# A third pair chunk in the gating stage, and later places for steps of the norms and of the conditioning sums

## The chip, the cores and the metric

The kernel runs on one core of one Trainium2 chip. The metric is the device time of one execution in microseconds (us); a smaller number is better. Of several executions the median is given.

## What is computed

The reference is one step of a two-layer streaming encoder on two inputs, a prompt of 1024 rows and a sample of 32 rows, all 1024 wide and in float32. In short, with the parts that this change touches:

```
mod = silu(c) @ w_ada[i] + b_ada[i]          # conditioning: shifts, scales, gates
h   = rmsnorm(x, g0) * (1 + sc1) + sh1
z   = gelu(h @ w_in);  u, v = split(z)        # 1024 -> 2 x 2048
v   = rmsnorm(v, g_v)
s   = einsum('gij,bnjgd->bnigd', w_s * mask, v) + b_s   # 8 groups, blocks of 128 rows
mix = (u * s) @ w_out                         # 2048 -> 1024   ("gating stage", layer 0)
x   = x + gt1 * rmsnorm(mix, g1)
h   = rmsnorm(x, g2) * (1 + sc2) + sh2
x   = x + gt2 * rmsnorm(square(relu(h @ w_up)) @ w_down, g3)   # 1024 -> 4096 -> 1024
```

Layer 1 has a pooling mixer in place of the gating. Outputs are the two results, and the state rows that the next step needs.

## The kernel before, in words

**Tiles.** The 1056 rows lie in three tiles, with rows on the free axis and features on the partitions: tiles 0 and 1 have 384 prompt rows each, tile 2 has 256 prompt rows and the 32 sample rows (288). `hh[t]`, `hl[t]` hold a tile's normalised input as two float32r halves, high and low, and every weight is split likewise: ScalarE rounds the high part (`wh`, line 592 or, in `w_split`, line 546), VectorE subtracts to get the low part (`wl`, through the helper at line 80). One product is then three matmuls: high by high, high by low, low by high (lines 1134 to 1136).

**The gating stage** (lines 1466 to 2043) works by groups. A group has 256 of the 2048 columns of u, that is two blocks of 128. An ordinary item (`sgu_item`) takes two groups for one tile: four products `up` (8 x 3 matmuls each), Gelu on ScalarE, for each group the 12 small matmuls of `spatial`, the gating on VectorE, the rounding `split` (lines 1453 to 1455), and later `down`: eight blocks of output, 4 x 3 matmuls each, which `accumulate` adds into `acc[t]` (the first one for a tile is copied by ScalarE). `down` is put on the list `pending` and given out after the first `up` of the item that follows.

**Pair chunks.** `upair_item` (chunk p has groups 2p and 2p+1) does tiles 0 and 1 together with seven products of half size where eight would be needed (`pair_item`, line 1667). It needs combinations of the weights' quarters (`quads`, line 550: from two weight loads come A1, S31, S24 and A22, with four VectorE passes over 128 x 512 and three and a half splits where the ordinary way has two) and combinations of the input's quarters (`combo`), which `u_sums` (line 1341) makes once, as a filler. Its last part, four steps that write over the first half of `hh[0]` and `hl[0]`, opens when the pair chunks begin ("h0"). For each half chunk the seven products run in a fixed order: A1, S31, S24, S24, S31, A1, A22; ScalarE copies four sums out of PSUM and VectorE makes three additions. The `down` of a pair chunk has 192 matmuls of 384 columns.

**Order.** `mixes` lists the ordinary items with their tiles, `UPAIRS` the pair chunks. Before: groups 4, 5 and then 6, 7 for tile 0; pair chunks 0 and 1 (groups 0 to 3, tiles 0 and 1); groups 0, 1 and then 2, 3 for tile 2; groups 4, 5 for tiles 1 and 2; groups 6, 7 for tiles 1 and 2. When the pair chunks are done, tile 0 is complete, and its norm, residual and next norm run beside the items that follow (`mix_to_ffn`, line 1912).

**One stream of loads.** All weights and the conditioning matrix come by one list, `stream`, in order, each load 512 KB into one of three `raw` buffers. `some_ada(n)` puts n loads of the conditioning matrix into the list; VectorE multiplies and adds these up (`do_ada`, line 654), and after every fourth a small matmul folds the sum over the partitions (`turn_sums`, line 683; `fold_lag` says how much later in the planner's time). Split weights have 16 places of 128 x 1024, two for a weight; six of them (`R`) are lent to the combinations until the pair chunks end.

**A planner.** While the program is written out, `time["pe"]` and `time["dve"]` count estimated TensorE and VectorE time. `weave` gives out the next steps of the stream and of the `fillers` (norms, residuals, sums) by them. A filler that yields a number waits for so many planned us. `Stat` is a norm's sum of squares: `split_sum` (line 956) makes its two halves, one on ScalarE; `finish` (line 1000) waits 3.0 planned us in the gating stage and 1.2 later, then gives out the ones-products `pn` (line 1005) and two ScalarE steps (lines 1009, 1010). Each engine works off its own list in order; `tc.issue_after(x)` keeps what its block gives out behind instruction x in the list of that engine. In the feed-forward part, `ffn_item` (line 1646) has Relu (line 1662), square (1664) and `split` on ScalarE for each `up`.

Of the kernel before, what the change touches and what calls it, by code (L numbers as in the profile page):

```python
# [11 lines left out]
AF = mybir.ActivationFunctionType  # L12
# [4 lines left out]
D = 1024  # L17
# [18 lines left out]
def tile_stream_encoder_step(  # L36
# [26 lines left out]
    act = nc.scalar.activation  # L63
# [6 lines left out]
    def tick(us):  # L70
        time["pe"] += us
        time["dve"] = max(time["dve"], time["pe"] - 4.0)
# [33 lines left out]
    def acc_tile(t):  # L106
# [19 lines left out]
        out=quad, in_=ident.rearrange("p (c m) -> p m c", m=32), op=ALU.add, axis=AX.X  # L126
# [4 lines left out]
    epsT = const.tile([P, 1], F32, name="eps")  # L131
# [15 lines left out]
    def ps_dn(name):  # L147
        return psum.tile([P, 512], F32, tag="pd", bufs=3, name=name)

    def ps_ms(name):  # L150
        return psum.tile([P, 512], F32, tag="pm", bufs=3, name=name)

    def t_m(name):
        return work.tile([P, 384], F32, tag="m", bufs=3, name=name)
# [191 lines left out]
    def w_groups(n):  # L346
        gs, _ = mixes[n]
        for g in gs:
            for k in range(2):
                f = 2 * g + k  # L350
                add_w(
                    ("u", n, g, k),
                    sgu_w_in[0][:, f * P : (f + 1) * P].rearrange("(k p) f -> p k f", p=P),
                    (8, P),
                )
        for q in range(2):
            for g in gs:
                add_w(
                    ("o", n, g, q),
                    sgu_w_out[0][g * 256 : (g + 1) * 256, q * 512 : (q + 1) * 512].rearrange(  # L360
                        "(k p) d -> p k d", p=P
                    ),
                    (2, 512),
                )

    def w_upair(p):
        for j in range(4):
            f = 4 * p + j
            add_w(
                ("up", ("u", p), j),  # L370
                sgu_w_in[0][:, f * P : (f + 1) * P].rearrange("(k p) f -> p k f", p=P),
                (8, P),
                ("one", "two")[j % 2],
            )
        for q in range(4):
            add_w(
                ("dn", ("u", p), q),
                sgu_w_out[0][p * 512 : (p + 1) * 512, q * 256 : (q + 1) * 256].rearrange(
                    "(j p) d -> p j d", p=P
                ),  # L380
                (4, 256),
            )
# [31 lines left out]
    every = list(range(NT))  # L414
# [5 lines left out]
    passes += [(1, c, PAIR, 1) for c in range(1, 8)]  # L420
    passes += [(1, c, [NT - 1], 2) for c in (0, 2, 4, 6)]
    LEND_AT = (("v", 1, 3), ("up", 0, 0))
    UPAIRS = (0, 1)

    rest = []

    def some_ada(n):
        for _ in range(min(n, len(rest))):
            add, l, j = rest.pop(0)
            add(l, j)  # L430
# [20 lines left out]
        some_ada(8)  # L451
    rest += [(add_wide, 1, j) for j in (*range(8, 16), *range(8), *range(16, 48))]

    mixes = [((4, 5), every[:1]), ((6, 7), every[:1]), ((0, 1), every[2:]), ((2, 3), every[2:])]
    mixes += [((4, 5), every[1:]), ((6, 7), every[1:])]
    for n in range(len(mixes)):
        w_groups(n)
        if n == 1:
            for p in UPAIRS:
                w_upair(p)  # L460
                some_ada(3)
        if n > 3:
            some_ada(5)
    for n, (l, c, tiles, m) in enumerate(passes):
        if tiles == PAIR:
            w_chunk(n, (1 if c < 3 else 2) if l else (5 if c == 1 else 6) if c < 7 else 1)
# [13 lines left out]
    landed = {}  # L480
    LANDING = 5.0
    last_copy = [None]

    def behind_copy():
        return ExitStack() if last_copy[0] is None else tc.issue_after(last_copy[0])
# [238 lines left out]
    fold_lag = [3.0]  # L724
# [165 lines left out]
    def finish(tag):  # L890
        while any(f[0] == tag for f in fillers):
            pull(True)
        time["pe"] = max(time["pe"], time["dve"] - 3.0)
# [26 lines left out]
    class Stat:  # L920
# [34 lines left out]

        def split_sum(self, sq):
            a, b = (x[:, : self.n] for x in self.parts)
            act(out=a, in_=sq, func=AF.Identity, bias=epsT)
            stt(out=b, in0=sq, scalar=epsT, in1=a.bitcast(F32), op0=ALU.add, op1=ALU.subtract)

        def square(self, k, src=None):
# [37 lines left out]

        def finish(self, out):  # L1000
            n = self.n
            yield 3.0 if gating_now[0] else 1.2
            pn = ps_ms(f"pn_{self.tag}")
            for i, x in enumerate(self.parts):
                mm(pn[:, :n], onesr, x[:, :n], start=i == 0, stop=i == 1)
            tick(0.4)
            q = t_m(f"q_{self.tag}")[:, :n]
            r = work.tile([P, 384], F32, tag="rr", bufs=2, name=f"r_{self.tag}")[:, :n]
            act(out=r, in_=pn[:, :n], func=AF.Abs_reciprocal_sqrt, scale=1.0 / D)
            act(out=q, in_=r, func=AF.Square)  # L1010
            yield 2.5
            stt(out=q, in0=pn[:, :n], scalar=-0.5 / D, in1=q, op0=ALU.mult, op1=ALU.mult)
            stt(out=r, in0=q, scalar=1.5, in1=r, op0=ALU.add, op1=ALU.mult)
            out.append(r)
            yield False


    gating_now = [True]
# [218 lines left out]
    with tc.manual_schedule():  # L1237
# [63 lines left out]
        ps = ps_ms("pv0_5")  # L1301
# [105 lines left out]
    for p, b in v_order:  # L1407
        ps = ps_dn(f"pv{p}_{b}")
# [42 lines left out]
            pending.pop(0)()  # L1451

    def split(dst_hi, dst_lo, src, n):
        act(out=dst_hi[:, :n], in_=src[:, :n], func=AF.Copy)  # L1454
        tt(out=dst_lo[:, :n], in0=src[:, :n], in1=dst_hi[:, :n].bitcast(F32), op=ALU.subtract)

    def accumulate(t, d, ps, first):
        n = ncol[t]
        if first:
            act(out=A(t, d), in_=ps[:, :n], func=AF.Copy)  # L1460
        else:
            tt(out=A(t, d), in0=A(t, d), in1=ps[:, :n], op=ALU.add)
# [113 lines left out]
    def sgu_item(p, t, mix, after):  # L1576
        gs, tiles = mixes[p]
        last = t == tiles[-1]
        n = ncol[t]
        hid = []  # L1580

        def put(g, k, s):
            a, b = t_hid("h", f"ush{g}_{t}_{k}"), t_hid("l", f"usl{g}_{t}_{k}")
            split(a, b, s, n)
            hid.append((a, b))

        inputs, factors, spatial, gate = gating(t, mix, put)
        us = []

        def up(g, k):  # L1590
            if k == 0:
                inputs(g)
            ps = ps_up(f"pu{g}_{t}_{k}")
            products(ps, n, up_terms(("u", p, g, k), t))
            if k == 0:
                factors(g)
            if last:
                w_finish(("u", p, g, k))
            u = t_m(f"u{g}_{t}_{k}")
            act(out=u[:, :n], in_=ps[:, :n], func=AF.Gelu_apprx_tanh)  # L1600
            us.append(u)

        def down():
            for d in range(KB):
                ps = ps_dn(f"po{gs[0]}_{t}_{d}")
                terms = []
                for j, (a, b) in enumerate(hid):
                    wh, wl = need_w(("o", p, gs[j // 2], d // 4))
                    o = (j % 2) * 512 + (d % 4) * P
                    terms.append((wh[:, o : o + P], wl[:, o : o + P], a[:, :n], b[:, :n]))  # L1610
                products(ps, n, terms)
                accumulate(t, d, ps, gs[0] == (4 if t == 0 else 0))
                if d == 0 and after is not None:
                    st = Stat(t, f"rs_{t}")
                if after is not None:
                    st.square(d)
                if last and d % 4 == 3:
                    for g in gs:
                        w_finish(("o", p, g, d // 4))
                weave(d % 2)  # L1620
            if after is not None:
                after(st)

        for j in range(4):
            up(gs[j // 2], j % 2)
            if j % 2 == 1:
                gate(gs[j // 2], spatial(gs[j // 2]), us)
            weave(2 if len(tiles) == 1 else 1)
            if j == 0:
                flush()  # L1630
        pending.append(down)

    more_hid = [None, 0]
# [78 lines left out]
    def pair_item(p, after, ends, gate=None):  # L1712
# [115 lines left out]
        def down():  # L1828
            sts = {}
            for q in range(4):  # L1830
                wh, wl = need_w(("dn", p, q))
                for t in tiles:
# [5 lines left out]
                    for d, ps in two:  # L1838
                        if wait == 4:
                            products(ps, n, [term(wh, wl, t, j, d) for j in range(4)])  # L1840
                        accumulate(t, d, ps, gate is not None and c == UPAIRS[0] and t > 0)
                        if t in ends:
# [146 lines left out]
    def upair_item(p):  # L1989
# [30 lines left out]
        gate["hook"] = hook  # L2020
        pair_item(("u", p), to_ffn0, [0] if p == UPAIRS[-1] else [], gate)

    def upairs():
        u_open.append("h0")
        need_w(("up", ("u", UPAIRS[0]), 0, "A1"))
        state["kept"] = 2
        for p in UPAIRS:
            upair_item(p)
# [4 lines left out]
        acc[NT - 1] = acc_tile(NT - 1)  # L2033

    for p, (gs, tiles) in enumerate(mixes):
        if p == 2:
            upairs()
        mix = {g: sgu_group(g) for g in gs}
        for t in tiles:
            sgu_item(p, t, mix, to_ffn0 if gs[-1] == 7 and t > 0 else None)  # L2040

    gating_now[0] = False
    sgu_stack.close()
    late = pool("late")

# [337 lines left out]
```

## Time and profile before

| | |
|---|---|
| three runs | 2097.35, 2098.18, 2099.37 us; median 2098.18 |
| the profiled execution | 2097.82 us, of which the span of instructions is 2096.0 |
| TensorE busy | 2075.2 us, 99% of the span |
| VectorE busy | 1636.7 us, 78% |
| ScalarE busy | 1060.3 us, 51% |
| granted TensorE clock | 0.999 |
| bytes moved | 303.91 MB, a mean of 145 GB/s |

The stages, by the first and last instructions of each in the trace: the v half ends at 222 us; ordinary items for tile 0 until the first pair chunk's first product at 278.1; pair chunks until 432.2; ordinary items until 608, where the first feed-forward product starts; from 676 on the pair chunks of the feed-forward part.

How to read it: PE is TensorE, PEld its weight loads, DVE is VectorE, ACT is ScalarE, SP issues most DMAs. Matmuls overlap, so the durations of single matmuls sum to more than the time that they take. "Idle before" is time in which an engine had nothing running, with what ended it.

### The profile page before, as it was taken

To read this page: it belongs to the slowest core of one execution; us is meant where nothing else is said; L and a number is where in the kernel's file an instruction comes from. 1 tells how busy PE (TensorE), PEld (TensorE's weight loads), DVE (VectorE), ACT (ScalarE), POOL (GpSimd) and SP (SyncE) were. 2 spreads that over 40 slices of the span, in tenths; PEclk is the share of its full clock that TensorE was granted. 3 is DMA by queue.
4 is the path that set the end of the run, shared out by engine and by line. 5 is a ranking of instruction groups with operands and counts; after the bars stand their busy time and mean duration, and the time that the engine had idled before them with its cause. 6 is when DMAs were issued, how large, how long until landed. Compare 5 with 4: busy or idle time off the path is not lost.

```text
span 2096.0 us, 32878 instructions
## 1 busy us (share of the span) xinstructions
PE 2075.2 (99%) x12742; PEld 2004.8 (96%) x12742; DVE 1636.7 (78%) x2953; ACT 1060.3 (51%) x1902; POOL 22.3 (1%) x44
## 2 busy tenths in 40 slices
PE   8999999999999999999999999999999999999998
PEld 6878999999999999999999999999999999999998
DVE  6799786889789998888868989896867654569554
ACT  5633443454247643344446766675435443365555
POOL 0000000000000000000000000000000000001100
PEclk9999999999999999999999999999999999999999
DMA  8585534365444443343424667643223221148863
GB/s 296 164 264 181 185 109 131 116 208 181 139 128 138 131 136 111 121 131 111 131 83 141 206 195 240 192 142 98 91 76 113 84 81 59 53 125 230 204 178 93
DMA packets 410737, 303.91 MB, mean 145 GB/s; under 512 B 47022, under 2 KB 373974, under 8 KB 410580
## 3 DMA queue, kind: packets, MB, share of 16 engines
q1 hardware_dynamic: 409652, 300.52, 47.4%
q8 instruction: 100, 1.64, 0.3%
q0 software_dynamic: 896, 1.28, 0.2%
q14 instruction: 57, 0.47, 0.1%
q10 hardware_dynamic: 32, 0.01, 0.0%
HBM read 271.09 MB, written 30.66 MB: 144 GB/s over the span
## 4 chain that ended last, share of the span: by engine, by line
PE 88%; DVE 7%; DMA 2%; ACT 2%; issue 1%; SPq 0%; DVEq 0%; ACTq 0%
PE pg L1135 11%; PE pg L1134 11%; PE pg L1136 11%; PE pf L1134 4%; PE pf L1136 4%; PE pf L1135 4%; PE pfa L1758 3%; PE pfa L1760 3%; PE pfa L1759 3%; PE pv L1160 2%; PE pv L1162 2%; PE pv L1161 2%; PE po L1134 2%; PE po L1135 2%; PE po L1136 2%; PE pu L1134 2%
## 5 line engine op out<-in xcount | busy, mean ns | idle before, releaser
L1134 PE MATMUL pg<-fh,wh_dn 128*128 128x384 f32 (+1 forms) x960 | 311.4, 325 | 1.4 <-ACT fh L1454 1.0
L1135 PE MATMUL pg<-fl,wh_dn 128*128 128x384 f32 (+1 forms) x960 | 310.4, 323 | 0.1
L1136 PE MATMUL pg<-fh,wl_dn 128*128 128x384 f32 (+1 forms) x960 | 309.9, 323 | 0.0
L80 DVE TENSOR_TENSOR acc<-acc,pg 128x384 f32<-128x384 f32 (+1 forms) x272 | 143.8, 533 | 106.0 <-PE pg L1136 105.4
L80 DVE TENSOR_TENSOR wl_dn<-raw,wh_dn 128x1024 fp32r<-128x1024 f32 x136 | 166.0, 1221 | 71.2 <-ACT wh_dn L592 43.0
L80 DVE SCALAR_TENSOR_TENSOR aa<-raw,csil,aa 128x512 f32<-128x512 f32 (+1 forms) x364 | 208.4, 619 | 6.3 <-DMA raw<-in_w_ada_dram 5.8
L1134 PE MATMUL pf<-hh,wh_up 128*128 128x288 f32 (+1 forms) x632 | 192.3, 305 | 0.0
L1135 PE MATMUL pf<-hl,wh_up 128*128 128x288 f32 (+1 forms) x632 | 191.1, 302 | 0.0
L1136 PE MATMUL pf<-hh,wl_up 128*128 128x288 f32 (+1 forms) x632 | 190.8, 302 | 0.0
L1134 PEld LDWEIGHTS pg<-fh,wh_dn 128*128 128x128 f32 x960 | 180.1, 188 | 3.0 <-ACT fh L1454 1.6
L592 ACT ACTIVATE wh_dn<-raw 128x1024 fp32r<-128x1024 f32 x136 | 143.7, 1057 | 75.2 <-PE pf L1135 34.0
L1135 PEld LDWEIGHTS pg<-fl,wh_dn 128*128 128x128 f32 x960 | 180.2, 188 | 1.0 <-DVE fl L80 0.6
L1136 PEld LDWEIGHTS pg<-fh,wl_dn 128*128 128x128 f32 x960 | 180.2, 188 | 0.0
L592 ACT ACTIVATE wh_up<-raw 128x1024 fp32r<-128x1024 f32 x79 | 83.6, 1058 | 79.0 <-PE pg L1135 46.0
L1136 PEld LDWEIGHTS pf<-hh,wl_up 128*128 128x128 f32 x632 | 118.9, 188 | 0.3 <-DVE wl_up L80 0.3
L1135 PEld LDWEIGHTS pf<-hl,wh_up 128*128 128x128 f32 x632 | 118.6, 188 | 0.5
L1134 PEld LDWEIGHTS pf<-hh,wh_up 128*128 128x128 f32 x632 | 118.5, 187 | 0.6 <-ACT wh_up L592 0.2
L80 DVE TENSOR_TENSOR wl_up<-raw,wh_up 128x1024 fp32r<-128x1024 f32 x79 | 96.4, 1220 | 28.7 <-ACT wh_up L592 28.7
L1134 PE MATMUL pg<-fx,wh_dn 128*128 128x288 f32 (+1 forms) x352 | 109.4, 311 | 0.2 <-ACT fx L1454 0.2
L1764 ACT ACTIVATE a<-pfa 128x384 f32<-128x384 f32 x84 | 40.9, 487 | 133.6 <-PE pfa L1760 133.5
L1135 PE MATMUL pg<-fx,wh_dn 128*128 128x288 f32 (+1 forms) x352 | 108.3, 308 | 0.0
L1136 PE MATMUL pg<-fx,wl_dn 128*128 128x288 f32 (+1 forms) x352 | 108.0, 307 | 0.0
(825 smaller groups left out, 5675.4 us busy)
## 6 DMA issues: line engine op xcount, KB each, us to landing
raw<-in_ffn_w_up_dram SPq DMA_DIRECT2D x136, 512.0 KB, 4.0
raw<-in_ffn_w_down_dram SPq DMA_DIRECT2D x136, 512.0 KB, 4.1
raw<-in_w_ada_dram SPq DMA_DIRECT2D x90, 512.0 KB, 4.2
raw<-in_sgu_w_in_dram SPq DMA_DIRECT2D x48, 512.0 KB, 4.4
raw<-in_sgu_w_out_dram SPq DMA_DIRECT2D x32, 512.0 KB, 3.6
xd<-acc SPq DMA_DIRECT2D x8, 1536.0 KB, 8.4
xo_r<-xd SPq DMA_DIRECT2D x32, 384.0 KB, 4.5
vd<-vt SPq DMA_DIRECT2D x32, 256.0 KB, 3.8
```

The lines of the kernel that those rows point to most:

```text
L80: return op(out, *args, **kw)
L592: act(out=wh, in_=r, func=AF.Copy)
L1134: mm(ps[:, :n], wh, rh, start=i == 0, stop=False)
L1135: mm(ps[:, :n], wh, rl, start=False, stop=False)
L1136: mm(ps[:, :n], wl, rh, start=False, stop=i == last)
L1160: mm(ps[:m, :], a_h, wh[:, o : o + 512], start=k == 0, stop=False)
L1161: mm(ps[:m, :], a_h, wl[:, o : o + 512], start=False, stop=False)
L1162: mm(ps[:m, :], a_l, wh[:, o : o + 512], start=False, stop=k == KB - 1)
L1758: mm(ps[:, :n], wh[:, o], rh, start=first and k == 0, stop=False, skip_group_check=True)
L1759: mm(ps[:, :n], wh[:, o], rl, start=False, stop=False, skip_group_check=True)
L1760: mm(ps[:, :n], wl[:, o], rh, start=False, stop=k == HK - 1, skip_group_check=True)
L1764: i = act(out=x, in_=ps[:, :n], func=AF.Copy)
```

## The change

Chunk 2 (groups 4 and 5, tiles 0 and 1) becomes a pair chunk. The ordinary items are now: 6, 7 for tile 0 before the pair chunks; then 0, 1, then 2, 3, then 4, 5 for tile 2; then 6, 7 for tiles 1 and 2. Behind each pair chunk's weights come four conditioning loads (three before), behind the last ordinary item's weights four (five behind each of the last two before): 16 in either kernel. `split` remembers its ScalarE rounding, and the ScalarE steps of `split_sum` and `finish` are given out behind the latest one. In the gating stage `finish` waits 5.0 planned us where it waited 3.0. From the end of the gating stage the conditioning folds wait 2.0 planned us where they waited 0.3. The flags for the first accumulation and for the start of the pair chunks follow the new order.

```diff
-    UPAIRS = (0, 1)
+    UPAIRS = (0, 1, 2)
...
-    mixes = [((4, 5), every[:1]), ((6, 7), every[:1]), ((0, 1), every[2:]), ((2, 3), every[2:])]
-    mixes += [((4, 5), every[1:]), ((6, 7), every[1:])]
+    mixes = [((6, 7), every[:1])] + [((g, g + 1), every[2:]) for g in (0, 2, 4)]
+    mixes += [((6, 7), every[1:])]
     for n in range(len(mixes)):
         w_groups(n)
-        if n == 1:
+        if n == 0:
             for p in UPAIRS:
                 w_upair(p)
-                some_ada(3)
-        if n > 3:
-            some_ada(5)
+                some_ada(4)
+        if n == 4:
+            some_ada(4)
...
+    last_hidden = [None]
+
+    def behind_hidden():
+        return ExitStack() if last_hidden[0] is None else tc.issue_after(last_hidden[0])
...
         def split_sum(self, sq):
             a, b = (x[:, : self.n] for x in self.parts)
-            act(out=a, in_=sq, func=AF.Identity, bias=epsT)
+            with behind_hidden():
+                act(out=a, in_=sq, func=AF.Identity, bias=epsT)
...
         def finish(self, out):
             n = self.n
-            yield 3.0 if gating_now[0] else 1.2
+            yield 5.0 if gating_now[0] else 1.2
...
-            act(out=r, in_=pn[:, :n], func=AF.Abs_reciprocal_sqrt, scale=1.0 / D)
-            act(out=q, in_=r, func=AF.Square)
+            with behind_hidden():
+                act(out=r, in_=pn[:, :n], func=AF.Abs_reciprocal_sqrt, scale=1.0 / D)
+                act(out=q, in_=r, func=AF.Square)
...
     def split(dst_hi, dst_lo, src, n):
-        act(out=dst_hi[:, :n], in_=src[:, :n], func=AF.Copy)
+        i = act(out=dst_hi[:, :n], in_=src[:, :n], func=AF.Copy)
+        last_hidden[0] = i.ins
...
-                accumulate(t, d, ps, gs[0] == (4 if t == 0 else 0))
+                accumulate(t, d, ps, gs[0] == (6 if t == 0 else 0))
...
-        if p == 2:
+        if p == 1:
             upairs()
...
     gating_now[0] = False
+    fold_lag[0] = 2.0
```

## The prediction

> **What bounds the kernel now.** I read the page first (busy times, chain), then a table of stretches, then TensorE's waits.
>
> ```profile
> span 2096.0 us, 32878 instructions
> PE 2075.2 (99%) x12742; PEld 2004.8 (96%) x12742; DVE 1636.7 (78%) x2953; ACT 1060.3 (51%) x1902; POOL 22.3 (1%) x44
> ...
> PE 88%; DVE 7%; DMA 2%; ACT 2%; issue 1%; SPq 0%; DVEq 0%; ACTq 0%
> ```
>
> TensorE is busy for 99% of the span, and 88% of the chain that ended last is its own. A change helps by giving it fewer matmuls or by closing one of its few gaps, and hurts by opening new ones. Stretches of the gating stage:
>
> ```profile
> core 0: us, PE busy (x) PEld busy (x) DVE busy (x) ACT busy (x) POOL busy (x), PEclk, DMA share, GB/s
> 220.70:297.20 76.50, 76.50 (x463) 75.16 (x462) 63.33 (x129) 35.16 (x57) 0.00 (x0) 1.00 0.51 158
> 297.20:363.17 65.97, 65.97 (x399) 65.90 (x398) 49.45 (x90) 25.92 (x45) 0.00 (x0) 1.00 0.38 118
> 329.89:363.17 33.28, 33.28 (x193) 33.28 (x193) 23.43 (x36) 9.78 (x16) 0.00 (x0) 1.00 0.45 137
> 432.00:517.00 85.00, 83.19 (x598) 82.12 (x597) 75.62 (x146) 46.38 (x70) 1.25 (x4) 1.00 0.67 209
> ```
>
> Up to the end of the pair chunks (432 us) TensorE has no gap in these stretches; behind them it loses 1.8 us of 85, while VectorE is busy for 75.6. The third row after the heading is the `down` of a pair chunk: 192 matmuls of 384 columns (and the end of one before) in 33.28 us, one per 0.1733 us. That is the price of a matmul here; the durations (334 ns in the trace) overlap and can't be summed. TensorE's gaps from all its waits:
>
> ```profile
> PE pg L1134 <- ACT fh L1454: 1.0, 1, 1.0
> PE pn_r_0x L1005 <- ACT sc_r_0x L958: 0.9, 1, 0.9
> ...
> PE pfa L1758 <- ACT a L1764: 0.7, 2, 0.5
> PE ada L710 <- DVE part L696: 0.6, 2, 0.3
> ```
>
> The first, second and fourth are those that the later steps bear on.
>
> **The change part by part.** *Third pair chunk.* For groups 4 and 5 and tiles 0 and 1, `up` was 2 tiles x 4 blocks x 24 = 192 matmuls; seven products for each of two halves are 14 x 12 = 168. `down`, `spatial` and the weight transposes keep their numbers. 24 fewer at 0.1733 us: **-4.16 us**. [...]
>
> *What it costs VectorE in the pairs.* Rows of the groups over the whole trace and over the first pair chunk:
>
> ```profile
> L80 DVE TENSOR_TENSOR raw<-raw 128x512 f32<-128x512 f32 x64 | 44.0, 687 | 0.9
> ...
> L80 DVE SCALAR_TENSOR_TENSOR aa<-raw,csil,aa 128x512 f32<-128x512 f32 x10 | 6.9, 745 | 0.0
> ```
>
> Two halves x (four passes of 0.69 + one and a half splits and three additions at 1.2 and 0.55, by rows below) = 12.4 us more VectorE work for the groups that change over, and one conditioning load more per chunk (four steps, about 2.9 us). The steady pair stretch has 49.5 of 66.0 us busy; 2.9 more makes 52.4, 79%. TensorE's matmuls hide it: 0, and a us for each above 66 if that cover went. ScalarE has 26 of 66. The chunk brings eight weight loads, the blocks of v and two groups' w_s and b_s to SP's queue, as many as the ordinary items did; the pair stretch has a DMA share of 0.38.
>
> *The handover into the first pair chunk.* Here the cover shrinks. Before, two ordinary items stand between the end of the v half and the first pair chunk; now one. The sums of the input's quarters must still be ready at the chunk's second product (`pfbu`, 297.11 before).
>
> ```profile
> L80 DVE SCALAR_TENSOR_TENSOR s<-psp,vec,bs 128x384 f32<-128x384 f32 x8 | 4.9, 612 | 4.6 <-PE psp L1531 4.6
> L80 DVE TENSOR_TENSOR usl<-s,ush 128x384 fp32r<-128x384 f32 x8 | 4.4, 550 | 0.1
> L80 DVE TENSOR_TENSOR s<-s,u 128x384 f32<-128x384 f32 x8 | 4.4, 548 | 0.0
> L80 DVE TENSOR_TENSOR acc<-acc,po 128x384 f32<-128x384 f32 x7 | 3.8, 549 | 0.1
> L80 DVE TENSOR_SCALAR wr<-wt,rv 128x128 f32<-128x128 f32 x12 | 3.0, 281 | 0.0
> L80 DVE SCALAR_TENSOR_TENSOR vst<-vst,rv,gvb 32x512 f32<-32x512 f32 x4 | 2.9, 733 | 2.9 <-DMA gvb<-in_sgu_g_v_dram 2.9
> ```
>
> ```profile
> 247.01 0.56 DVE L80 TENSOR_TENSOR usum_x<-hh,hl 128x384 f32<-128x384 f32 x1
> ...
> 255.33 0.54 DVE L80 TENSOR_TENSOR combo_r<-usum_z,combo_r 128x384 fp32r<-128x384 f32 x1
> ...
> 262.97 2.36 DVE L80 TENSOR_TENSOR wl_o<-raw,wh_o 128x1024 fp32r<-128x1024 f32 x2 [1.24 <-ACT wh_o L592]
> ...
> 280.37 0.55 DVE L80 TENSOR_TENSOR usum_v<-hh,hl 128x384 f32<-128x384 f32 x1
> ...
> 291.29 0.55 DVE L80 TENSOR_TENSOR hl<-usum_u,hh 128x384 fp32r<-128x384 f32 x1
> 292.83 1.28 DVE L80 TENSOR_TENSOR wl_up_('u', 0)_0_S<-raw,wh_up_('u', 0)_0_S 128x512 fp32r<-128x512 f32 x2
> ...
> 297.11 0.33 PE L1758 MATMUL pfbu<-hh,wh_up_('u', 0)_0_S 128*128 128x384 f32 x1
> ```
>
> From 220.7 to 297.2 VectorE is busy for 63.3 us. The item that goes takes 8 low halves (two in 2.36, so 1.18 each: 9.4), half of the gating rows ((4.9 + 4.4 + 4.4 + 3.0) / 2 = 8.4, 0.7 more for its two transposes) and 3.8 of additions, now first copies on ScalarE: 22.3 by busy sums, some 20 since neighbours overlap. TensorE's time shrinks by 192 x 0.1733 + 24 spatial matmuls (two blocks of 12 in 1.34 each, below) = 36.0. So 41 to 43 us of work stand in 40.5 us. The four `vst` (2.9) are a filler behind the sums and can come later; 38.5 to 40.5 then remain, beside about 2 us that VectorE waits at the start for the first group. The sums of 247.0 to 255.3 and 280.4 to 291.3 (11 and 16 steps) fall together into the time of one `down`. The rounded S31 was ready at 294.1, 3 us before it was needed; that cushion takes most of it. Bounds: below, 0; above, nothing overlaps better: 43.3 + 2 + 2.9 - 40.5 = 7.7 us, the cushion gone. I take **+1.5**, near the lower end, as only the sums are in the path.
>
> *Norms behind the rounding, later ones-products.*
>
> ```profile
> 472.59 0.30 PE L1136 MATMUL pu<-hh,wl_u 128*128 128x288 f32 x1
> 472.73 0.38 PE L1485 MATMUL wsT<-ident,wt 128*128 128x128 f32 x2
> 473.97 0.44 PE L1005 MATMUL pn_r_0x<-sc_r_0x,ones 128*128 128x384 f32 x1 [0.87 <-ACT sc_r_0x L958]
> ```
>
> ```profile
> 643.70 0.45 PE L1005 MATMUL pn_r_1x<-sm_r_1x,ones 128*128 128x384 f32 x1
> 645.13 0.44 PE L1134 MATMUL pg<-fh,wh_dn 128*128 128x384 f32 x1 [0.99 <-ACT fh L1454]
> ```
>
> ```profile
> 642.28 0.62 ACT L958 ACTIVATE sc_r_1x<-sq_r_1x,eps 128x384 fp32r<-128x384 f32 x1 [2.88 <-DVE sq_r_1x L80]
> 642.80 0.47 ACT L1662 ACTIVATE r<-pf 128x384 f32<-128x384 f32 x1
> ...
> 644.18 0.49 ACT L1009 ACTIVATE r_r_1x<-pn_r_1x 128x384 f32<-128x384 f32 x1 [0.35 <-PE pn_r_1x L1005]
> 644.57 0.51 ACT L1454 ACTIVATE fh<-r 128x384 fp32r<-128x384 f32 x1
> ```
>
> At 642 ScalarE stands idle for 2.88 us before `sc_r_1x`, which waits for VectorE, and Relu, square and rounding of the feed-forward block stand behind it: TensorE starts `pg` at 645.13, 1.43 after the last `pn`, where 0.17 is the pace. With the norm's step behind that rounding, the block's three steps run in the idle time: -1.2. The norm's step itself can't start before VectorE's sum either way, so its ones-product loses nothing here. At 473.97 `pn` waits for its half: 0.87 us, and two planned us more in `finish` put it behind further products: -0.9. The conditioning folds' 0.6 goes with the longer lag. Queued behind each new edge are the norm's own VectorE steps alone, and these end in a norm that has time (tile 0's is needed when the feed-forward part starts, four items of 28.6 us and one of 36 on). Bounds of these three: -2.7, and above +2 if the new places open gaps as large as those closed, as each `pn` that stands before its half is ready stops TensorE. I take **-2.2**.
>
> *Three items of tile 2 in a row.* The stage after the pair chunks keeps its work but for one tile-1 item and six conditioning loads, which went ahead. I take **+0.3**.
>
> Sum: -4.16 + 1.5 - 2.2 + 0.3 = -4.6. The profiled execution took 2097.8 (span 2096.0 and 1.8 around it), so 2093.2 by its own time; the median of the runs stands 0.36 above it. I forecast **2093.6 us** for the median.
>
> **The rivals.** *1. The handover stalls.* If `vst` or the second group's gating comes ahead of the sums, TensorE waits 5 to 7.7 us at the second pair product instead of 1.5: 2097.1 to 2099.8, and 2097.5 as its time. For it: VectorE at about 100% for 40 us. Against: the stretch's last rows show the cushion, and the S24 weights alone depend on it at once.
>
> *2. Tile 2's weights come late (slower).* Behind the pair chunks three items of 288 columns follow each other, each with eight weights.
>
> ```profile
> 230.88 1.34 PE psp L1531 x12
> ...
> 428.13 1.06 ACT L592 ACTIVATE wh_u<-raw 128x1024 fp32r<-128x1024 f32 x1 [0.99 <-PE pgu L1136]
> ...
> 459.21 1.05 ACT L592 ACTIVATE ring<-raw 128x1024 fp32r<-128x1024 f32 x1
> ...
> 479.98 1.06 ACT L592 ACTIVATE wh_u<-raw 128x1024 fp32r<-128x1024 f32 x1 [0.54 <-DMA raw<-in_sgu_w_in_dram]
> ```
>
> An item takes 192 x 0.135 (the start of 472.73 is 0.14 after 472.59) + 2 x 1.34 = 28.6 us, 3.6 us a weight. Sixteen high halves start from 428.13 to 479.98: 3.46 us each, and the last five, beside tile 0's norm, 5.2 apart. Before, a tile-1 item followed two such items and let the stream catch up; now a third one follows. The mechanism decides at 3.6 + 9/24 = 4.0 us a weight, where 24 weights lose 9 us, more than twice the gain; at 4.1, near the mean of both stretches (2.8 and 5.2), it is 12 us: 2093.6 + 12 = 2105.6. Against it: the five far apart may wait for places, not for data, and the conditioning loads that stood behind them are gone. [...]
>
> *3. The later steps close nothing.* The planner's time is an estimate, and every gap moves when 32 us of work are reordered; the gaps would be others, of the same sum: -4.16 + 1.8 = -2.4, 2095.8. For it: the gaps are single ones, each by chance of place.
>
> **How the numbers follow.** About 0.2% (4.2 us) is what a measurement of this kernel can tell from no change, so faster is below 2094.0 and slower above 2102.4. Forecast 0.55 (its own range 2089.5 to 2096, three quarters of it faster); rival 1, 0.16; rival 2, 0.13; rival 3, 0.16 (a fifth of it faster). Faster: 0.41 + 0.02 from rival 1 + 0.03 from rival 3 = 0.46. Slower: 0.12 from rival 2 + 0.02 from rival 1 with a worse order than priced = 0.14. Same: 0.40. The range runs from three gaps closed, no stall at the handover, and also `pfa`'s 0.7 and the other 0.9 of the 1.8 us lost from 432 to 517 gone (2098.2 - 4.2 - 2.7 - 0.7 - 0.9 = 2089.7, so 2089.5) to rival 2 at its threshold, 2103.
>
> **What would show it.** TensorE's matmul count must fall by 24 (the records can miss some). Right: `pfbu` of the first chunk starts within 2 us of the `po` before it; no gap at the first feed-forward `down`; weights of tile 2 before their products. Wrong: waits of `pfau` or `pfbu` on `wl_up`, `combo` or `hh` near 262; of `pu` on `wl_u` from 465 to 550; `pn` rows with waits of 1 us or more.

## The result and the profile after

The changed kernel takes **2102.48 us** (median of 20 runs, 2099.20 to 2107.53), the kernel before 2098.43 us beside it (20 runs). The ratio is 1.0022, with a 95% interval of 1.0016 to 1.0028: by that ratio some 4.6 us slower (4.05 by the medians), where 4.6 us faster was forecast. The profiled execution took 2102.62 us, its span is 2100.8, 4.8 more than before. Line numbers of the changed kernel are a few higher: the products stand in lines 1141 to 1143, `split` in 1461, the ones-products in 1011, root and square of `finish` in 1016 and 1017, Relu and square of the inner blocks in 1670 and 1672.

The page of the changed kernel:

```profile
span 2100.8 us, 32874 instructions
PE 2075.2 (99%) x12718; PEld 2001.4 (95%) x12718; DVE 1648.6 (78%) x2973; ACT 1066.6 (51%) x1916; POOL 22.3 (1%) x44
```

TensorE has exactly 24 matmuls fewer, 12718 for 12742. It stands idle for 25.6 us (span less busy) where it stood 20.8. And its busy time, which 24 x 0.173 us should have shortened by 4.2, is the same 2075.2. The table of stretches shows where the idle time is; first the kernel before, then the changed one (columns: stretch, its length, then for each engine busy us and the instructions that ran in it; then granted clock, DMA share, GB/s):

```profile
470.00:610.00 140.00, 139.12 (x953) 138.08 (x952) 120.50 (x246) 50.12 (x80) 1.25 (x4) 1.00 0.50 154
...
1160.00:1240.00 80.00, 79.83 (x557) 75.42 (x556) 72.37 (x108) 55.76 (x96) 0.00 (x0) 1.00 0.71 210
```

```profile
470.00:610.00 140.00, 136.34 (x981) 134.59 (x980) 118.86 (x240) 68.15 (x106) 1.56 (x5) 1.00 0.60 182
...
1160.00:1240.00 80.00, 77.86 (x538) 74.10 (x537) 69.57 (x101) 52.40 (x89) 0.00 (x0) 0.98 0.69 207
```

Two stretches hold the idle time that is new: 470 to 610, behind the pair chunks (3.66 us where it was 0.88), and 1160 to 1240, at the change to the second layer (2.14 where it was 0.17). Along the pair chunks themselves (280 to 470) it is 0.99 us where it was 0.92. In the last row the granted clock is 0.98. The waits of TensorE in the changed kernel (total, number, longest, in us) name the places:

```profile
PE pg L1141 <- ACT fx L1461: 1.9, 1, 1.9
...
PE pn_r_0x L1011 <- ACT sc_r_0x L964: 1.5, 2, 1.3
...
PE po L1141 <- ACT ush L1461: 1.2, 1, 1.2
PE pn_r_1x L1011 <- DVE sm_r_1x L80: 1.1, 1, 1.1
```

The second and third are at 509 and 520 us, the fourth at 638, in the place of the 1.0 that `pg` waited for `fh` at 645. The first, at 1216.85, is new and costs more than its own length. TensorE there, and the granted clock around it:

```profile
1214.48 0.29 PE L1141 MATMUL pg<-fx,wh_dn 128*128 128x288 f32 x1
1214.61 0.29 PE L1142 MATMUL pg<-fx,wh_dn 128*128 128x288 f32 x1
1216.85 0.55 PE L1141 MATMUL pg<-fx,wh_dn 128*128 128x288 f32 x1 [1.95 <-ACT fx L1461]
1217.20 0.44 PE L1143 MATMUL pg<-fx,wl_dn 128*128 128x288 f32 x1
1217.44 0.44 PE L1141 MATMUL pg<-fh,wh_dn 128*128 128x288 f32 x1
```

```profile
479.66:483.07 3.41, 2.38 (x19) 2.04 (x17) 2.02 (x5) 1.33 (x3) 0.00 (x0) 1.00 0.83 226
1213.53:1216.94 3.41, 1.46 (x11) 1.12 (x9) 3.36 (x5) 3.27 (x6) 0.00 (x0) 1.00 1.01 326
1216.94:1220.35 3.41, 3.41 (x15) 3.41 (x16) 1.88 (x4) 0.99 (x2) 0.00 (x0) 0.50 1.03 345
```

Ahead of the wait a matmul of 288 columns starts every 0.13 us, behind it every 0.24: for 3.41 us the clock is at half. Fourteen matmuls start in that time, each 0.107 us later than at full clock, which is 1.5 us; half of the 3.41 would be 1.7. So one wait of 2.1 us (from one start to the next, less the pace) costs some 3.7. The first row is another stretch of the same length, with TensorE busy for 2.38 us of it, and no half clock follows. The half clock is also why TensorE's busy time did not fall by 4.2: 1.5 to 1.7 of it is slow matmuls. Most of the rest should be the ends of matmuls ahead of new waits, which count as busy for their whole 0.3 us and not for the pace; that is argued, not shown.

What ScalarE and VectorE did ahead of that wait, in the changed kernel:

```profile
1213.32 0.85 ACT L975 ACTIVATE sq_r_1x<-acc 128x768 f32<-128x768 f32 x1 [2.97 <-DVE acc L80]
1214.07 0.39 ACT L1670 ACTIVATE r<-pf 128x288 f32<-128x288 f32 x1
...
1215.30 0.43 ACT L1672 ACTIVATE r<-r 128x288 f32<-128x288 f32 x1
...
1216.37 0.43 ACT L1461 ACTIVATE fx<-r 128x288 fp32r<-128x288 f32 x1
```

```profile
1212.32 0.96 DVE L80 TENSOR_TENSOR acc<-acc,xo_r 128x768 f32<-128x768 f32 x1 [0.51 <-DMA xo_r<-xd]
```

A norm's square stands at the head of ScalarE's list and waits 2.97 us for the residual's sum on VectorE; Relu, square and rounding of the block that TensorE needs next stand behind it.

### The profile page after: what moved, and what is told of

It is laid out like the page before. It is cut to its first block, busy times and chain, and to the rows that moved or that the text cites. A ratio compares the mean times of both kernels' runs of the same rounds, so it can differ in the third digit from the quotient of the medians.

```text
span 2100.8 us, 32874 instructions
## 1 busy us (share of the span) xinstructions
PE 2075.2 (99%) x12718; PEld 2001.4 (95%) x12718; DVE 1648.6 (78%) x2973; ACT 1066.6 (51%) x1916; POOL 22.3 (1%) x44
```

## The experiments

Two theories stood at the start. **T**: the 24 products are saved, tile 2's three items in a row make weights late, and one late load at 1212 makes the wait at 1217; the later steps have no part in it. **R**: the later steps themselves, the order on ScalarE above all, make the new gaps. All ratios below are to the kernel before on the same chip, with 95% intervals; each kernel has 5 to 11 runs.

**The chunk alone.** The changed kernel without the three later steps:

```diff
-            with behind_hidden():
-                act(out=a, in_=sq, func=AF.Identity, bias=epsT)
+            act(out=a, in_=sq, func=AF.Identity, bias=epsT)
...
-            yield 5.0 if gating_now[0] else 1.2
+            yield 3.0 if gating_now[0] else 1.2
...
-            with behind_hidden():
-                act(out=r, ...); act(out=q, ...)
+            act(out=r, ...); act(out=q, ...)
...
-    fold_lag[0] = 2.0
```

> The new pair chunk with its order of the gating items and its flags, without the three later steps (no order on ScalarE, ones-product 3.0 behind, folds 1.0 behind). The 24 products less are worth 24 x 0.1733 = 4.16 us. Theory T (24 products are saved, but three tile-2 items in a row make weights late, about 3.5 us between 470 and 610, and a residual's load at 1,212 lets TensorE wait 2.1 us, behind which the clock is at half for 3.4 us): the losses at 470 to 610 stay, the wait at 1,217 hangs on loads and may stay too, so the time is that of the changed kernel within 3 us, 2,099 to 2,104. Rival R (the later steps make the new gaps): without them the losses at 470 to 610 and at 1,217 are gone and the time is that of the kernel before less 4.2: 2,093 to 2,096. A half clock that shows at another place than 1,217 would say that it is a matter of chance which wait is long enough.

Measured: 2101.72 us, ratio 1.0009 (1.0000 to 1.0018); the folds wait 0.3 here, as in the kernel before, and not the 1.0 of the expectation. The time is in T's range and above R's. From 470 to 610 TensorE is idle for 3.54 us, and from 1160 to 1240 for 0.16:

```profile
470.00:610.00 140.00, 136.46 (x986) 134.83 (x984) 119.12 (x239) 70.19 (x108) 1.56 (x5) 1.00 0.60 184
...
1160.00:1240.00 80.00, 79.84 (x561) 75.79 (x560) 72.29 (x108) 55.87 (x95) 0.00 (x0) 1.00 0.71 211
```

Each theory has a half: the loss behind the pair chunks belongs to the chunk and its order of items, the one at 1217 to the later steps. The chunk by itself gains nothing: it was to bring 2.4 us.

**The later steps alone**, on the kernel before (ScalarE's order, 5.0, folds at 2.0; `mixes` and `UPAIRS` as before).

> The kernel before with the three later steps alone (ScalarE's order, ones-product 5.0 behind, folds 2.0 behind). Theory T: the gaps only move, 2,097 to 2,100 unless a wait of 2 us trips the half clock. Rival R: the later steps cost, so the time is about 4 to 8 us above that of the kernel before, 2,102 to 2,106, and the wait at 1,217 is there. My own step on record, -2.2 us for the later steps, would give 2,095 to 2,097.

Measured: 2099.24 us, ratio 1.0001 (0.9992 to 1.0010), in T's range and not in R's 2,102 to 2,106. The wait at 1217 is here too, 1.95 us lost from one start to the next at 1214.65, without a half clock in the profiled execution:

```profile
1210.70:1214.10 3.40, 2.17 (x17) 1.93 (x15) 3.35 (x5) 2.98 (x5) 0.00 (x0) 1.00 0.91 275
1214.10:1217.50 3.40, 2.85 (x21) 2.84 (x22) 2.74 (x6) 1.81 (x4) 0.00 (x0) 1.00 1.07 393
```

So the later steps open this wait in either order of the items, and T's last part is wrong. At 645 they gain 0.69 us (the loss is 0.57 for 1.26). On the kernel before, wait and gain together can't be told from nothing.

**Without the order on ScalarE.** The changed kernel with both `behind_hidden()` taken out, the 5.0 and the folds kept.

> The changed kernel without the order on ScalarE between the norm's steps and the rounding. Theory T: at 1,217 ScalarE's square waits for the residual's load, which no edge touches, so the wait and the half clock stay: 2,101 to 2,104, and the 1.26 us gap at the first gate product of an inner block is back near 645 in the place of the 1.37 us gap at 638. Rival R (edges hold ScalarE): about 3 to 4 us less, 2,098 to 2,100, and no half clock at 1,217.

Measured: 2098.14 us, ratio 0.9995 (0.9987 to 1.0004). R's number: in the changed kernel the order on ScalarE costs 0.0027, some 5.7 us. The wait at 1217 is gone (idle 0.14 us from 1160 to 1240), and so is the gap at 638. The gap at 645, which T had expected back, is not there either: with the new order of the items the ones-product of that norm starts some ten us earlier (633.55 for 643.70), so no order on ScalarE is needed for it.

**The squares ordered too.** Since a square headed ScalarE's list at 1213:

```diff
-            act(out=sq..., in_=..., func=AF.Square)
+            with behind_hidden():
+                act(out=sq..., in_=..., func=AF.Square)
```

> The changed kernel with the norm's squares on ScalarE also put behind the inner block's rounding, as its other ScalarE steps are. At 1,213 that square stood 3 us before a load with Relu, the fold's square and the rounding behind it. Theory T: the square no longer stands ahead of them, the 2.1 us wait at 1,217 and the half clock behind it go: -3.8 us, 2,097.5 to 2,100 if no other square becomes late. Rival: the wait comes back as a wait of the rounding's or of the norm itself elsewhere, and the time stays at 2,101 to 2,104.

Measured: 2102.30 us, ratio 1.0015 (1.0006 to 1.0024). TensorE still waits 1.4 us for `fx` (1.55 lost at 1215.56). The profiled execution has no half clock, but the median stays, in the rival's range: the square is where the delay shows, not where it comes from.

**Which of the two orders.** Root and square alone (first), the eps step alone (second).

> The changed kernel with ScalarE's order only at the norm's root and square, not at its eps step. Theory E: at 1,141 the root r_rf stands behind a rounding and comes 1 us later, VectorE's queue waits for it, and VectorE, which has no time left until 1,211, passes that on to the residual at 1,212; so this half of the order makes the 2 us wait at about 1,216: 2,101 to 2,103. Rival: the eps step's order makes it, the wait is gone here: 2,097.5 to 2,099.

Measured: 2103.07 us, ratio 1.0019 (1.0010 to 1.0028), with 2.02 us lost at 1221.18 (its traced execution took 2107.87 us, and all that is behind 490 is shifted by some 4 us).

> The changed kernel with ScalarE's order only at the norm's eps step, not at its root and square. Theory E (root and square make the wait at 1,216): no such wait here, 2,097.5 to 2,099.5, and the eps step behind a rounding moves the gap at 638 only. Rival: the wait at about 1,216 is there, 2,101 to 2,103.

Measured: 2098.72 us, ratio 1.0002 (0.9993 to 1.0010), with 0.52 us lost there and no half clock. TensorE's waits in the kernel with root and square ordered, then in the one with the eps step ordered:

```profile
PE pg L1140 <- ACT fx L1460: 1.9, 1, 1.9
...
PE pn_r_1x L1010 <- DVE sm_r_1x L80: 1.1, 1, 1.1
```

```profile
PE pg L1140 <- ACT fx L1460: 0.4, 1, 0.4
```

Root and square it is. They make a second gap too, the one at 638, which the expectation above gave to the eps step. By starts of matmuls it is 1.37 to 1.40 us in the three kernels of the changed order of items that have root and square ordered, and it is missing from the four without. With 2.1 us at 1217 and some 1.6 for the half clock that is 5.1 of the 5.7 us. How the wait at 1217 comes about shows at 1140 us. First ScalarE and VectorE without the order, then with it; TensorE runs 3.03 us later in the changed kernel from 1100 to 1157 (`pg` at 1097.05 and 1100.08), so 3.03 is to be added to the first.

```profile
1137.89 0.48 ACT L1014 ACTIVATE r_rf<-pn_rf 128x384 f32<-128x384 f32 x1
...
1138.59 0.52 ACT L1015 ACTIVATE q_rf<-r_rf 128x384 f32<-128x384 f32 x1
1139.01 0.44 ACT L1459 ACTIVATE fh<-r 128x288 fp32r<-128x288 f32 x1
```

```profile
1139.14 0.56 DVE L80 SCALAR_TENSOR_TENSOR q_rf<-pn_rf,q_rf 128x384 f32<-128x384 f32 x1 [0.19 <-ACT q_rf L1015]
...
1140.92 1.14 DVE L80 SCALAR_TENSOR_TENSOR acc<-acc,coef,r_rf 128x384 f32<-128x384 f32 x2
```

```profile
1141.53 0.44 ACT L1461 ACTIVATE fh<-r 128x288 fp32r<-128x288 f32 x1
1141.88 0.85 ACT L1016 ACTIVATE r_rf<-pn_rf 128x384 f32<-128x384 f32 x2
1142.62 0.94 ACT L1017 ACTIVATE q_rf<-r_rf 128x384 f32<-128x384 f32 x2
```

```profile
1143.18 1.02 DVE L80 SCALAR_TENSOR_TENSOR q_rf<-pn_rf,q_rf 128x384 f32<-128x384 f32 x2 [0.72 <-ACT q_rf L1017]
...
1145.05 1.22 DVE L80 TENSOR_TENSOR wl_up<-raw,wh_up 128x1024 fp32r<-128x1024 f32 x1
1146.19 0.45 DVE L80 TENSOR_TENSOR fl<-r,fh 128x288 fp32r<-128x288 f32 x1
1146.56 0.61 DVE L80 SCALAR_TENSOR_TENSOR acc<-acc,coef,r_rf 128x384 f32<-128x384 f32 x1
```

Without the order the first root runs between Relu and the inner block's square, at 1140.92 by the changed kernel's clock. With it both roots stand behind the rounding, at 1141.88. VectorE's list waits 0.72 us for the root's square; its step on that square starts 1.0 us late (1143.18 for 1142.17), and the first sum that needs the norm 2.6 us late (1146.56 for 1143.95). The other 1.6 us come from VectorE's own list, which has another order now: a weight's low half (`wl_up`), which stood behind the first two sums, stands ahead of them, and so does the last step of the other tile's norm (at 1144.58, without the order at 1159.90). From there to 1211 VectorE has next to no idle time to make it good:

```profile
1147.00:1211.00 64.00, 63.81 (x480) 63.57 (x480) 62.43 (x92) 47.10 (x81) 0.00 (x0) 1.00 0.72 212
```

The residual's sum is 2.2 us late at 1212.32 (1207.12 + 3.03 = 1210.15 would have been in time), 70 us behind the cause. T's load is in it, but does not make the wait: here VectorE stands idle for 0.51 us until the residual has landed, 4.6 us behind its issue where the kernel without the order has 3.6. In the kernel with root and square alone, and in the kernel before with the later steps, the load lands in 3.6 and 3.7 us, VectorE does not wait for it, and TensorE's wait is there all the same. That the order of root and square makes the wait is shown by these two runs; the way through VectorE's list is read from the rows.

**The ones-product early again**, without ScalarE's order:

```diff
-            yield 5.0 if gating_now[0] else 1.2
+            yield 3.0 if gating_now[0] else 1.2
```

> The changed kernel without ScalarE's order and with the ones-product 3.0 instead of 5.0 behind in the gating stage; the folds stay later. The chunk alone stood at 1.0009 of the kernel before, with the later product and folds at 0.9995: 2.9 us for both. If the folds make it (the ada fold at 1,032 lost 0.72 with the folds early): 2,098 to 2,099. If the ones-product makes it: about 2,100. My step on record gave the later product 0.9 us at 474; in the changed kernel the gap at that product is 1.38 to 1.44 us with 5.0 and 1.37 with 3.0, so at that place it would be nothing.

Measured: 2098.90 us, ratio 1.0003 (0.9995 to 1.0012). The interval overlaps with that of the kernel that has 5.0, and the loss at `pn_r_0x` is 1.38 us in either: the later ones-product does nothing at its place. Between the chunk alone and the kernel without ScalarE's order lie 0.0014; by the ratios 0.0008 of them belong to the ones-product, by the medians most (2.8 of 3.6 us) to the folds. The intervals settle neither.

**Another order of the items**, without ScalarE's order: the two-tile item moved between tile 2's items. (The flag that starts the last norms follows the new order; that line is left out here.)

```diff
-    mixes = [((6, 7), every[:1])] + [((g, g + 1), every[2:]) for g in (0, 2, 4)]
-    mixes += [((6, 7), every[1:])]
+    mixes = [((6, 7), every[:1]), ((0, 1), every[2:]), ((6, 7), every[1:])]
+    mixes += [((g, g + 1), every[2:]) for g in (2, 4)]
```

> The changed kernel without the order on ScalarE, and with another order of the gating items after the pair chunks: tile 2's item of groups 0 and 1, then the two-tile item of groups 6 and 7, then tile 2's items of groups 2 and 3 and of 4 and 5 (three single items in a row before). Without ScalarE's order alone, 470 to 610 lost 5.4 us against 2.5 in the kernel before, at pn_r_0x 1.38 (508 us), po 1.16 (519) and psp 0.46 (481). Theory A (weights come too fast one after another): the two-tile item gives time between, 470 to 610 falls to about 3 us, and the time is 2 us under that of the kernel without ScalarE's order, 2,095 to 2,097. Rival: the losses come from the norm of tile 0 and the gating's first step behind the chunks, at the same places in any order; the time stays at 2,097 to 2,099.

Measured: 2105.11 us, ratio 1.0025 (1.0014 to 1.0036): neither theory's number. The losses went up, in the traced execution of 2110.29 us to 3.4 us at 583 (`psp` behind VectorE's `wr`) and 3.6 at 625 (the first inner block's weight), with half clocks behind both. At 625:

```profile
622.25:625.66 3.41, 0.66 (x10) 0.42 (x10) 3.41 (x7) 1.06 (x1) 0.00 (x0) 1.00 0.35 106
625.66:632.49 6.83, 5.97 (x26) 5.87 (x25) 6.40 (x13) 2.70 (x5) 0.00 (x0) 0.50 0.73 218
```

While TensorE waits there, VectorE is busy for all 3.41 us and the DMA engines for 35%. At 583 it is not so: from 577.87 to 581.29 VectorE is busy for 0.46 us and waits for ScalarE. What both places share is a weight's load for which ScalarE waits 4.13 us at the head of its list. Why the loads are late, for want of a free buffer or otherwise, is not shown.

**Tile 0's norm later.** The residual and norm of tile 0 begin, without ScalarE's order, when the third of tile 2's items begins, and in a second kernel with the two-tile item:

```diff
     def mix_to_ffn(st, l):
...
+        while l == 0 and t == 0 and item_now[0] < 3:
+            yield 1.0
```

> The changed kernel without ScalarE's order, and with tile 0's residual and norm (its ones-product, four loads of the residual, its store, squares and second ones-product) begun only when the third tile-2 item begins, at about 533, and not at about 486. At 500 to 520 the DMA engines were 98 to 99% busy (298 and 290 GB/s) and ScalarE waited for weights up to 2.1 us; at 550 to 600 they were 36% busy. Theory A (traffic and VectorE work of tile 0's residual and of the weights of three single items meet at 480 to 520): the losses at 508 (1.38) and 519 (1.16) go, 470 to 610 falls from 5.4 to about 3, and the time is 2 to 2.5 us under that of the kernel without ScalarE's order, 2,095.5 to 2,097. Rival: the weights alone fill the DMA, and the gap at the ones-product moves with the norm: 2,097.5 to 2,099.

> The same with tile 0's residual and norm begun with the two-tile item, at about 558. Theory A: the losses at 508 and 519 are gone as well, but the norm of tile 0 meets that of tile 1 before the inner blocks at 620, so up to 2 us come back between 600 and 650: 2,095.5 to 2,099. Rival (weights alone): 470 to 520 keeps its losses, 2,098 to 2,101.

Measured: 2103.52 us, ratio 1.0021 (1.0012 to 1.0030), and 2105.98 us, ratio 1.0035 (1.0021 to 1.0049). Both times lie above every expected range. The first half of theory A holds: the losses at 508 and 519 are gone. Without the delay, and with it (first kernel):

```profile
500.00:510.00 10.00, 8.78 (x67) 8.44 (x66) 9.81 (x18) 4.91 (x7) 0.93 (x3) 1.00 0.98 298
510.00:520.00 10.00, 9.00 (x70) 8.77 (x69) 8.79 (x19) 5.11 (x10) 0.00 (x0) 1.00 0.99 290
```

```profile
500.00:510.00 10.00, 10.00 (x80) 10.00 (x79) 6.61 (x14) 5.59 (x9) 0.00 (x0) 1.00 0.71 212
510.00:520.00 10.00, 10.00 (x79) 9.84 (x78) 7.96 (x20) 4.31 (x9) 0.00 (x0) 1.00 0.71 209
```

The DMA engines fall from 98% to 71%, and TensorE has no gap. But VectorE now has idle time here, and lacks it later. In the same delayed kernel at 660:

```profile
660.42 1.01 PE L1139 MATMUL pf<-hh,wh_up 128*128 128x384 f32 x2 [4.34 <-ACT hh L1099]
```

```profile
656.97:660.38 3.41, 0.00 (x0) 0.00 (x0) 3.41 (x7) 1.85 (x6) 0.00 (x0) 1.00 0.75 256
660.38:663.79 3.41, 3.37 (x10) 2.93 (x11) 3.41 (x7) 1.91 (x4) 0.00 (x0) 0.50 0.19 67
```

Tile 1's input is 4.3 us late, VectorE is busy without a break, and a half clock follows: the gain is given back with interest.

**A smaller delay** (`item_now[0] < 2`), and **the later steps without root and square** on the kernel before:

> As the kernel with tile 0's residual and norm begun with the third tile-2 item, but begun one item earlier, with the second (at about 508 in the place of about 486). Begun at 533, the losses at 508 and 519 were gone and 4.5 us with a half clock came back at 660, where tile 1's input of the inner blocks was late: VectorE had stood idle for some 10 us more between 490 and 530. Theory A (the work given later needs VectorE's idle time, which here is lost for half as long): the loss at 508 goes, that at 519 stays in part, and at 660 0 to 2 us come back: 2,096.5 to 2,100. Rival (the residual's loads at 508 to 530 meet the next item's weights as before): the losses move by 22 us and keep their size, 2,098 to 2,100, and nothing comes back at 660.

> The kernel before with the later steps but without the one that proved dear: eps step behind the rounding, ones-product 5.0 behind, folds 2.0 behind; root and square where they were. My step on record put these at -2.2 us less what root and square were to bring. With root and square moved too, the same kernel stood at 1.0001 with 1.95 us lost at 1,215. If that wait was all that the later steps cost and their gains are real (645 from 1.26 to 0.57, 1,032 from 0.38 to nothing): 2,096.5 to 2,097.5. If the gains belong to other shifts of the same work and come and go: 2,098 to 2,099.5.

Measured: 2096.54 us, ratio 0.9992 (0.9983 to 1.0000), the lowest time of all, though its interval touches 1 and it can't be told from the kernel without ScalarE's order (0.9995); and 2098.81 us, ratio 0.9999 (0.9990 to 1.0008). With the small delay the losses at 508 and 519 are gone, nothing comes back at 660, and 470 to 610 has 1.85 us idle for 2.78. Its profile has a loss of 2.15 us at 702 (`pfa` for a copy on ScalarE) that the others have with 0.6 to 1.2; why, stays open. The last kernel shows no gain of the remaining later steps on the kernel before: it keeps the whole loss at 645 (1.26 us at 646.22), and the wait at 1217 is gone (idle 0.04 us from 1160 to 1240). Nor can its 0.9999 be told from the 1.0001 with root and square ordered too: the price of 5.7 us is that of the changed order of items, where the gap at 638 and the half clock are added, and was not seen on the kernel before.

## Why the prediction was wrong, step by step

The forecast was 9.2 us off, and two parts share this almost evenly. The chunk with its order of items was to bring -4.16 + 1.5 + 0.3 = -2.4 us and stood at +0.0009, 1.9 us. The later steps were to bring -2.2 and added the other 0.0013, 2.7 us: the order on ScalarE 5.7, against 2.9 by which the kernel with later folds and ones-product but without that order lies under the chunk alone. (Some of these intervals overlap, so the split is rough.) That 2102.48 lies inside the stated range, close to its upper end, is luck: that end was 9 us of late weights without any cost of the later steps, and what came was some of the one and some of the other.

- **24 matmuls fewer, -4.16:** right; the count fell by 24. By starts of matmuls less the usual pace of their form, TensorE's losses behind 80 us grew from 36.5 to 45.7 us, which with -4.16 gives +5.0 beside a span that grew by 4.8.
- **The handover, +1.5:** the first `pfbu` starts at 260.54, 0.17 behind the last `po`, with no gap; the waits come later, 0.67 at 299 and 0.32 at 301. From 280 to 470 TensorE is idle for 0.99 us where it was 0.92, and by starts of matmuls 220 to 470 loses 1.0 us more: inside the bounds, and a little below the term.
- **Norms behind the rounding, later ones-products, -2.2: the step that failed.** It was to close gaps at 645, 474 and in the folds, up to +2 at worst. The changed kernel without ScalarE's order is some 5.7 us faster than the one with it. Two things were wrong. First, the order keeps a step behind the *latest rounding given out so far*, not behind the next one. The eps step at 642 was to go behind a rounding that is given out after it, and it did not move: with the later steps on the kernel before, ScalarE still waits 2.88 us at its head, with Relu, square and rounding behind. Only the root, given out later, changed places with the rounding; that is the 0.69 us gained at 645, and the kernel before that has the eps step ordered, but not root and square, does not gain it:

```profile
641.79 0.62 ACT L964 ACTIVATE sc_r_1x<-sq_r_1x,eps 128x384 fp32r<-128x384 f32 x1 [2.88 <-DVE sq_r_1x L80]
...
643.37 0.52 ACT L1461 ACTIVATE fh<-r 128x384 fp32r<-128x384 f32 x1
643.80 0.47 ACT L1016 ACTIVATE r_r_1x<-pn_r_1x 128x384 f32<-128x384 f32 x1
```

  Second, "Queued behind each new edge are the norm's own VectorE steps alone" fails at 1140: VectorE's list behind a late root holds the next residual and the weights as well, and this norm has no time to spare. The prediction goes through the gating stage and the first inner blocks and never through the change of layers, though the edit works in every norm.
- **Three items of tile 2 in a row, +0.3: mis-sized.** It measured +2.8 us of idle time from 470 to 610 (0.88 to 3.66; 3.9 by starts of matmuls), and 2.7 in the chunk alone: the greater part of what the chunk's terms missed. It is near rival 2, late loads, and far below the 9 us at which that would have decided, but not by its sign: TensorE does not wait for `wl_u`. At 520 it waits for `ush`, which stands in ScalarE's list behind a rounding that waited 1.93 us for its weight's load. Weights and tile 0's residual meet there at 98% DMA share (in the kernel without ScalarE's order), and with the residual delayed the losses at 508 and 519 went.
- **Rival 3** (gaps only move) fits the later ones-product and the folds, of which no gain is clear of the noise: the gap at `pn_r_0x` stays at 1.38 us, and the fold at 1032 loses 0.7 us again in the kernel with the eps step ordered, in spite of the later folds. It missed the price of the order.
- **The half clock** has no term in the sum. It came at a wait of 2.1 us in the changed kernel, and cost 1.5 to 1.7.

## What to carry to other kernels

An order between two instructions on one engine is to be followed to the engine that waits for the later one: a step moved back by 1 us on ScalarE held VectorE's list and let other work ahead of the norm's, and VectorE, with 1.6 us idle in the next 64, handed the delay to TensorE 70 us on. A gap can be moved out of one stretch only into idle time of the engine that does the work; read that engine's busy time where the work is to go before moving it. And check in code what an order is tied to, the last such instruction given out or the next one, for every place where the helper runs.

## What the runs showed of the hardware

A TensorE wait of 2 us cost nearly twice its length at one place (2.1 and some 1.6 us at 1217 in the changed kernel) and was followed by no half clock at another: in the kernel with the later steps alone, where 1.95 us are lost at 1214.65, TensorE is busy for 2.17 and 2.85 us in the two rows of 3.40 there, and the granted clock is 1.00 in both and from 1160 to 1240. Ten half clocks stand in the rows of these traces from 480 to 1230 us: nine last 3.41 us and one 6.83. In the three kernels with more than one, their starts lie 737.28 us apart (485.22 and 1222.50, root and square ordered), 98.98 and 40.96 (485.72, 584.70 and 625.66, the other order of items) and 143.35 (485.27 and 628.62, tile 0's norm begun with the two-tile item), which are 216, 29, 12 and 42 times 3.413 (40.96 / 12). The rows of the first of these kernels, each half clock behind the 3.41 us ahead of it:

```profile
481.81:485.22 3.41, 1.98 (x16) 1.63 (x14) 1.43 (x5) 1.51 (x3) 0.00 (x0) 1.00 0.91 277
485.22:488.63 3.41, 3.41 (x15) 3.41 (x16) 3.41 (x8) 1.53 (x3) 0.00 (x0) 0.50 0.55 182
1219.09:1222.50 3.41, 1.55 (x11) 1.31 (x10) 3.36 (x5) 2.04 (x4) 0.00 (x0) 1.00 1.04 358
1222.50:1225.91 3.41, 3.41 (x16) 3.41 (x16) 2.44 (x5) 1.83 (x3) 0.00 (x0) 0.50 1.04 338
```

In the ten rows of 3.41 us just ahead of a half clock, each with the granted clock at 1.00, TensorE was busy for 1.46 us (the changed kernel), 1.98 and 1.55 (root and square ordered), 1.60 (the ones-product early), 1.93, 1.78 and 0.66 (the other order of items), 0.00 (tile 0's norm begun with the third item), 0.81 and 1.87 (begun with the two-tile item). Busy time alone does not sort them: in the kernel without ScalarE's order TensorE is busy for 1.94 us of the 3.40 from 1597.00, and the clock is 1.00 there and in the 3.40 us behind. What sets a half clock off is not shown. Nor is it shown whether such stretches come at other places in other executions of the same kernel and make its runs spread by 1.7 us and more: the granted clocks of 0.995 to 0.999 in the changed kernel's 20 runs would fit that, but only one execution of each kernel has a trace.
